# A hybrid recurrent decoder layer on one core: the first norm's squares on TensorE, the S5 tables in the opening, the S5 sums on all partitions

## The chip, the cores and the metric

One core of a Trainium2 chip runs the whole kernel. The metric is device microseconds of one execution, taken as the median of several runs. Shares and rows come from one profiled execution of the same program. Its engines are TensorE (PE, with its weight loads shown as PEld), VectorE (DVE), ScalarE (ACT), GpSimd (POOL) and SyncE (SP), which issues the DMAs.

## The reference

One decoder layer is computed for 1024 new positions of a prompt and for 8 single new tokens (1032 columns, features on the partitions). What matters here is the first half of the layer:

```
mod = silu(c) @ ada_w + ada_b                   # six parts of 1024: sh1, sc1, g1, sh2, sc2, g2
hn = x * rsqrt(mean(x*x) + eps) * norm1_g * (1 + sc1) + sh1
proj = hn @ w_in                                # 1024 x 1536: lru_x, lru_gate, s5_u
conv  = width-4 causal convolution of lru_x;  hs = gated real scan of conv (RG-LRU)
S5: 32 groups of 16 channels, each with one 64-dim complex diagonal state
  bu = Bbar u;  h[t] = abar * h[t-1] + bu[t]  (complex);  y = Re(C h) + d*u;  gelu, GLU
merged = [rmsnorm(hs * gelu(lru_gate)), rmsnorm(s5)];  x += g1 * (merged @ w_out)
```

Then follow a second modulated norm, a SwiGLU block of width 2816, and the final norm. States at the end of the sequence are outputs too.

## The kernel before, in words

Every fp32 product of the projections is made of three matmuls: a weight and an activation are each split into a high and a low part (`hnh`, `hnl`, `wh`, `wl`; lines 142 to 144), and the columns go in three pieces of 344. TensorE's instructions run in the order in which the code issues them, in the whole kernel.

**The opening** (lines 593 to 683) has its order written out by hand for every engine. It loads x in eight 128-row blocks and the scale part of `ada_w` in four quarters. For each pair of blocks (loop `i`, `d = 2 * i`), ACT and DVE split two columns of weights (`split_w01`) and form the modulated x (`stage`: ACT makes `hnh`, DVE makes `hnl`, POOL the eight token columns). ACT squares x (`square`, line 546). TensorE runs the products of these blocks with the first two column tiles of `w_in` (`first`) and the dot product that gives the next quarter of the scale (`ada_dot`, `ada_sum` in `scale_out`). The norm's factor is applied after the product, so the sum of squares is only needed near the end: POOL adds squares into `sqs[0]` in the loop (`add_square`), DVE does the last three adds, and `rstd_sums` sums over partitions with four TensorE matmuls against ones, one for each strip of 258 columns, into one of the two `small` PSUM banks. ACT takes the root and DVE the reciprocal. The steps of small S5 tables (`s5_powers`, some 80 tiny instructions) are pumped in between on DVE.

**The units** (from line 1089). Behind the opening come 30 units of 24 matmuls: one column tile of `w_in` times one third of the columns. `at(i, fn, ...)` hangs other work in front of unit `i`. DVE, ACT, POOL and SP are there ordered by a planner that works with estimated costs; TensorE keeps the order of the code. The S5 half goes in four tiles `f_`, with `STARTS = (4, 9, 14, 19)`: input tables, output tables (`s5_out_tables`) and the rotation `et` (`s5_rot`, on POOL) before the start; then `s5_turn`, `s5_drive` in two halves one and two units later, `s5_toeplitz` two units later, and `s5_out` five and seven units later. The second drive calls `s5_state`: rotate, scan, rotate back, all on DVE. Where an S5 result changes from channels on partitions (two groups of 64) to real and imaginary rows on partitions, the last subtraction or addition was made on 64 partitions at a time, two instructions for each (`ost` and `xt`), and one 4-element instruction more for the final state (`fin`, line 940).

The rotation tables `etb` and `eta` are made on POOL in front of unit 1, by 42 tensor_tensor instructions and four memsets; `lru_decay_scale` (32 dependent DVE instructions on 128x4) stands in front of unit 4. Its results `cl` and `ncl` are first read after the last unit, by `lru_exp`.

From the last unit on: gates, scans and GLU, then the output projection, and from about a third of the span on the SwiGLU block, whose products are made with fewer multiplications (bank names X, Y, Z).

Of the kernel before, what the change touches and what calls it, by code (L numbers as in the profile page):

```python
# [9 lines left out]
F32 = mybir.dt.float32  # L10
# [3 lines left out]
ALU = mybir.AluOpType  # L14
# [4 lines left out]
P = 128  # L19
# [35 lines left out]
def body(ctx, tc, a, o):  # L55
# [12 lines left out]
    def tt(out, x, y, op, e=None):  # L68
        (e or V).tensor_tensor(out=out, in0=x, in1=y, op=op)  # L69

    def mul(out, x, y, e=None):
        tt(out, x, y, ALU.mult, e)

    def add(out, x, y, e=None):
        tt(out, x, y, ALU.add, e)
# [468 lines left out]
    def square(d):  # L544
        sqs.append(f(f"sq1_{d}", TT))
        S.activation(sqs[d], xs[d][:, 0:TT], AF.Square)

    def add_square(d, e=None):
        add(sqs[0], sqs[0], sqs[d], e)

    def first(d, m, cs=range(NC)):
        for c in cs:
            mm3(banks[m, c], wcols(w01[m], d), cols(hn[d], c), d == 0, d == DK - 1)
# [35 lines left out]
    def split_w01(i, m):  # L589
        wh, wl = (t.rearrange("p (k n) -> p k n", k=DK)[:, 2 * i:2 * i + 2] for t in w01[m])  # L590
        split(wh, wl, w01_raw[:, 2 * i:2 * i + 2, m])

    small_a = [s5_angles()]
    small_b = [s5_powers()]

# [28 lines left out]
    first(1, 1)  # L624
    scr_ = cp.tile([P, 3], F32, name="scr")
    scr, scr2, scr3 = (scr_[:, i:i + 1] for i in range(3))
    for i in range(1, 4):
        d = 2 * i
        split_w01(i, 0)
        split_w01(i, 1)  # L630
        stage(d)
        stage(d + 1)
        if i == 1:
            pump(small_a, 99)
            pump(small_b, B1)
        elif i == 2:
            S.activation(scr, epst, AF.Sqrt)
        for j in ((1,), (2, 3), (4,))[i - 1]:
            add_square(j, G)
        if i < 3:  # L640
            sb = ada_dot(s_raw[i + 1], f"s{i + 1}")
        first(d, 0)
        square(d)
        if i < 3:
            scale_out(i + 1, *sb)
        square(d + 1)
        first(d, 1)
        first(d + 1, 0)
        if i < 3:
            first(d + 1, 1)  # L650
        if i < 3:
            pump(small_b, B0)
    add(sqs[6], sqs[6], sqs[5])
    add(sqs[6], sqs[6], sqs[7])
    add_square(6)
    split_in2 = split_w(w_in[2], "in2", pool=fp, tags=("F", "F"))
    for c in range(NC):
        evac(0, c, banks[0, c], True)
# [4 lines left out]
    rsb = dict(enumerate(sh_raw))  # L663
    rb1 = f("rb1", TT)
    bank20 = in_bank("in2_0", 0)
    r1 = rstd_sums((sqs[0],), D, "n1", TT, 4, f)
    for _ in steps(bank20, split_in2, [in_cols(hn[k], 0) for k in range(DK)]):
        pass
    pump(small_b, B2)
# [60 lines left out]
    def behind_states():  # L730
        return tc.issue_after(state_ends[-1]) if state_ends else nullcontext()

    etb = sp.tile([P, 2, 16, 16], F32, name="etb")
    eta = sp.tile([P, 2, 16, 8], F32, name="eta")

    def tpl(name):
        return sp.tile([P, 4, P], F32, tag="tpl", bufs=1, name=name)

    def s5_rot_tables(tab, k0, n):
        G.memset(tab[:, 0, :, 0:1], 1.0)  # L740
        G.memset(tab[:, 1, :, 0:1], 0.0)
        m = 1
        for k in range(n):
            er = rot[:, 0, k0 + k].unsqueeze(2).to_broadcast([P, 16, m])
            ei = rot[:, 1, k0 + k].unsqueeze(2).to_broadcast([P, 16, m])
            lo_, hi_ = tab[:, :, :, 0:m], tab[:, :, :, m:2 * m]
            for o_, x, y, op in ((0, er, ei, ALU.subtract), (1, ei, er, ALU.add)):
                w = tpl(f"te{k0}_{k}_{o_}").rearrange("p a b -> p (a b)")[:, 0:16 * m]
                w = w.rearrange("p (q m) -> p q m", q=16)
                mul(hi_[:, o_], lo_[:, 0], x, G)  # L750
                mul(w, lo_[:, 1], y, G)
                tt(hi_[:, o_], hi_[:, o_], w, op, G)
            m *= 2


    fin = sp.tile([P, 2, 16, 9], F32, name="fin")

    def s5_fin():
# [47 lines left out]
    def s5_out_tables(f_):  # L806

        q0 = 4 * f_
        cr, ci = sq[f_]["bc"][:, 1, 0], sq[f_]["bc"][:, 1, 1]
        awr = apw[:, 0, q0:q0 + 4].unsqueeze(3).to_broadcast([P, 4, 9, 16])  # L810
        awi = apw[:, 1, q0:q0 + 4].unsqueeze(3).to_broadcast([P, 4, 9, 16])
        crb = cr.unsqueeze(2).to_broadcast([P, 4, 9, 16])
        cib = ci.unsqueeze(2).to_broadcast([P, 4, 9, 16])
        ost = sp.tile([P, 8, 144], F32, tag="ost", bufs=2, name=f"ost{f_}")
        ov = ost.rearrange("p (q g) k -> p q g k", g=2)
        for ri, x, y in ((0, crb, cib), (1, cib, crb)):
            w = [t4(f"cw{ri}{i}_{f_}") for i in range(2)]
            wv = [t.rearrange("p q (j c) -> p q j c", j=9) for t in w]
            mul(wv[0], awr, x)
            mul(wv[1], awi, y)  # L820
            for g2 in range(2):
                h = slice(g2 * 64, g2 * 64 + 64)
                if ri == 0:
                    sub(ov[0:64, :, g2], w[0][h], w[1][h])
                else:
                    stt(ov[64:128, :, g2], w[0][h], -1.0, ALU.mult, w[1][h], ALU.subtract)
        sq[f_].update(ost=ost)

    def s5_rot(f_):
# [82 lines left out]
    def s5_state(f_):  # L912

        q0, pr = 4 * f_, sq[f_]
        vt, et = pr["vt"], pr["et"]
        add(fin[:, :, q0:q0 + 4, 1:9], fin[:, :, q0:q0 + 4, 1:9], vt[:, :, :, 0:8], G)
        w = [t4(f"rw{i}_{f_}")[:, :, 0:P] for i in range(3)]
        vr, vi = vt[:, 0, :, 8:136], vt[:, 1, :, 8:136]
        mul(w[0], et[:, 0], vr)
        mul(w[1], et[:, 1], vi)  # L920
        add(w[0], w[0], w[1])
        mul(w[1], et[:, 0], vi)
        mul(w[2], et[:, 1], vr)
        sub(w[1], w[1], w[2])
        for ri in range(2):
            for q in range(4):
                V.tensor_tensor_scan(out=vt[:, ri, q, 8:136], data0=mag8[:, q0 + q:q0 + q + 1].to_broadcast([P, P]),
                                     data1=w[ri][:, q], initial=0.0, op0=ALU.mult, op1=ALU.add)
        xt_ = sp2[0].tile([P, 8, 136], F32, tag="xt", bufs=1, name=f"xt{f_}")
        G.memset(xt_[:, :, 0:1], 0.0)  # L930
        nc.sync.dma_start(out=xt_[:, :, P:136], in_=a["h0s"][:, 8 * f_:8 * f_ + 8])
        xv = xt_.rearrange("p (q g) k -> p q g k", g=2)
        for ri, x, y, op in ((0, vr, vi, ALU.subtract), (1, vi, vr, ALU.add)):
            w = [t4(f"dw{ri}{i}_{f_}")[:, :, 0:P] for i in range(2)]
            mul(w[0], et[:, 0], x)
            mul(w[1], et[:, 1], y)
            for g2 in range(2):
                h = slice(g2 * 64, g2 * 64 + 64)
                tt(xv[64 * ri:64 * ri + 64, :, g2, 1:P], w[0][h, :, 0:P - 1], w[1][h, :, 0:P - 1], op)
            pr["last"] = V.tensor_tensor(out=fin[:, ri, q0:q0 + 4, 0:1], in0=w[0][:, :, P - 1:P],  # L940
                                         in1=w[1][:, :, P - 1:P], op=op)
            state_ends.append(pr["last"].ins)
        pr["xt"] = xt_

    def s5_out(f_, half):
# [97 lines left out]


    R0, R1 = 4, 1.12
    STARTS = (4, 9, 14, 19)
    IT, OT, RT, TZ, DA, DB, OA, TN, OB = 5, 0, 1, 2, 1, 2, 3, 1, 2
    CLOSE = 27
    before, mids = {}, {}
# [19 lines left out]
    at(2, bias_dot)  # L1069
    mids[1] = {1: [(rest_out, (3,))]}  # L1070
    mids[2] = {0: [(first_done, ())]}
    at(4, pump, [lru_decay_scale()], 99)
    for j in range(4, 20):
        i = int(R0 + R1 * (j - 4))
        at(i, rest_load, j)
        at(i + 2, rest_dot, j)
        at(i + 3, rest_out, j)
    at(1, s5_rot_tables, etb, 1, 4)
    at(1, s5_rot_tables, eta, 5, 3)
    at(3, s5_fin)  # L1080
    for f_ in range(4):
        i0 = STARTS[f_]
# [11 lines left out]
    for i, (m, c) in enumerate(SEQ):  # L1094
        for fn, args in before.get(i, []):
            fn(*args)
        if i == CLOSE:
            s5_end()
            s5ctx.close()
            hp = ctx.enter_context(tc.tile_pool(name="hp", bufs=15))  # L1100
            hpool.append(hp)
            gy_raw = [gy_load(f_) for f_ in range(4)]
        if (m, c) == (11, 2):
            wabf = wp.tile([P, 2, 4, P], F32, tag="wf", bufs=2, name="wabf")
            G.memset(wabf, 0.0)
            for j, nm in enumerate(("wa", "wx")):
                for e in range(2):
                    nc.sync.dma_start(out=wabf[e * 64:(e + 1) * 64, j, :, e * 64:(e + 1) * 64], in_=a[nm][e])
        if (m, c) == (11, 0):
            w_glu0 = load_w(a["w_glu"][0], "glu0")  # L1110
        if (m, c) == (2, 0):
            w_cur[3] = split_w(w_in[3], "in3")
        elif c == 2 and 3 <= m < 11:
            w_cur[m + 1] = load_w(a["w_in"][m + 1], f"in{m + 1}")
        b = in_proj(m, c, w_cur[m], mids.get(i, {})) if i else bank20
        if m < 4:
            u_out(m, c, b)
        elif m < 8:
            lx_out(m - 4, c, b)
        else:  # L1120
            gt_out(m - 8, c, b)
# [791 lines left out]
```

## Time and profile before

| | |
|---|---|
| median of 3 runs | 1166.81 us (1165.96 to 1168.72) |
| profiled execution: time, span | 1164.8 us, 1162.8 us |
| mean granted TensorE clock | 0.968 |
| PE, PEld busy | 94%, 90% |
| DVE, ACT, POOL busy | 73%, 43%, 39% |
| chain that ended last, shares | PE 70%, DVE 17%, ACT 5%, issue 4%, POOL 2%, DMA 1% |

A busy share is over the whole span; a busy matmul or DVE instruction may itself have been held up. The granted clock is in parts of the full one: 1.0 is 2.4 GHz, and a stretch whose mean lies between 0.5 and 1.0 was partly at 1.2 GHz. In rows of the timeline the first number is the start, the second the length, and the brackets hold the idle time of that engine before the row and what ended it.

### The profile page before, as it was taken

What the parts mean: (1) busy time and instruction counts of PE and PEld (TensorE: products, weight loads), DVE (VectorE), ACT (ScalarE), POOL (GpSimd) and SP (SyncE); (2) the same over time, 40 slices, a digit from 0 to 9 for tenths busy, and PEclk for the clock granted to TensorE, in tenths of its full rate; (3) what the DMA queues carried; (4) which work ended last, traced back from release to release, by engine and by line L of the source; (5) the groups of instructions that cost most, each with busy time, mean ns of one, the idle gap of its engine ahead of it and who ended that gap; (6) DMA issues with size and microseconds to landing.
All of it is one profiled execution on the core that took longest, in us unless ns stands there. A gap on an engine that the chain in (4) does not pass through costs nothing.

```text
span 1162.8 us, 21429 instructions
## 1 busy us (share of the span) xinstructions
PE 1088.8 (94%) x8480; PEld 1042.0 (90%) x8480; DVE 843.9 (73%) x1360; ACT 499.8 (43%) x948; POOL 456.3 (39%) x475
## 2 busy tenths in 40 slices
PE   7887889999987999899999999999999999999995
PEld 5776778896977998799999999999999999999995
DVE  6879799853978268986677687667645367778966
ACT  4433324327765145664445454445444521221253
POOL 3396645301020004574655575466432142233022
PEclk9898989899998999899999999999999999999998
DMA  9557455423042313052543344234313967459212
GB/s 344 183 155 206 156 171 146 154 77 107 19 130 89 130 56 110 19 193 90 192 182 129 109 182 155 101 146 182 128 56 102 350 259 303 171 202 294 89 54 93
DMA packets 90627, 174.92 MB, mean 150 GB/s; under 512 B 18720, under 2 KB 54304, under 8 KB 90528
## 3 DMA queue, kind: packets, MB, share of 16 engines
q1 hardware_dynamic: 90528, 173.57, 43.1%
q8 instruction: 66, 1.08, 0.4%
q14 instruction: 33, 0.27, 0.1%
HBM read 126.56 MB, written 46.98 MB: 149 GB/s over the span
## 4 chain that ended last, share of the span: by engine, by line
PE 70%; DVE 17%; ACT 5%; issue 4%; POOL 2%; DMA 1%; SPq 0%; DVEq 0%; ACTq 0%; POOLq 0%
PE X L1510 9%; PE X L1511 9%; PE X L1512 9%; PE Y L1510 5%; PE Y L1511 5%; PE Y L1512 5%; PE o L1308 2%; PE o L1309 2%; PE o L1310 2%; PE Z L1511 2%; PE Z L1512 2%; PE Z L1510 2%; DVE rw L69 1%; PE in L142 1%; PE in L143 1%
## 5 line engine op out<-in xcount | busy, mean ns | idle before, releaser
L69 POOL TENSOR_TENSOR u<-u,p 128x258 f32<-128x258 f32 x44 | 41.9, 953 | 125.2 <-ACT u L1562 115.8
L142 PE MATMUL in<-hnh,wh_in 128*128 128x344 f32 (+1 forms) x240 | 83.1, 346 | 0.0
L143 PE MATMUL in<-hnl,wh_in 128*128 128x344 f32 (+1 forms) x240 | 80.1, 334 | 0.0
L144 PE MATMUL in<-hnh,wl_in 128*128 128x344 f32 (+1 forms) x240 | 80.1, 334 | 0.0
L69 POOL TENSOR_TENSOR st_d<-wf_d 128x256 f32<-128x256 f32 x32 | 26.2, 838 | 111.6 <-PE X L1512 42.7
L69 POOL TENSOR_TENSOR sa_g<-wf_g 128x512 f32<-128x512 f32 x11 | 14.8, 1344 | 123.1 <-PE o L1310 91.4
L69 DVE TENSOR_TENSOR acc<-X,acc 128x258 f32<-128x258 f32 x128 | 49.9, 420 | 10.4 <-PE X L1512 10.2
L142 PEld LDWEIGHTS in<-hnh,wh_in 128*128 128x128 f32 x240 | 48.2, 201 | 2.9 <-issue 2.9
L143 PEld LDWEIGHTS in<-hnl,wh_in 128*128 128x128 f32 x240 | 48.1, 200 | 0.0
L144 PEld LDWEIGHTS in<-hnh,wl_in 128*128 128x128 f32 x240 | 47.7, 199 | 0.0
L1562 ACT ACTIVATE u<-X 128x258 f32<-128x258 f32 x88 | 33.1, 381 | 31.4 <-PE X L1512 31.4
L69 DVE TENSOR_TENSOR hs<-v,hs 128x516 fp32r<-128x516 f32 x32 | 46.1, 1458 | 0.6 <-ACT hs L1380 0.6
L1309 PE MATMUL o<-ls,wh_s 128*128 128x258 f32 x128 | 37.4, 292 | 5.6 <-DVE ls L69 5.6
L1308 PE MATMUL o<-hs,wh_s 128*128 128x258 f32 x128 | 37.3, 291 | 0.0
L1310 PE MATMUL o<-hs,wl_s 128*128 128x258 f32 x128 | 37.3, 291 | 0.0
L1308 PE MATMUL o<-hl,wh_l 128*128 128x258 f32 x128 | 36.6, 286 | 0.0
L69 POOL TENSOR_TENSOR acc<-acc,rbf 128x388 f32<-128x388 f32 x10 | 11.9, 1218 | 62.9 <-ACT rbf L201 51.1
L87 DVE SCALAR_TENSOR_TENSOR xz<-o,mod,xz 128x258 f32<-128x258 f32 (+1 forms) x32 | 15.2, 480 | 29.2 <-PE o L1310 25.6
L1310 PE MATMUL o<-hl,wl_l 128*128 128x258 f32 x128 | 36.1, 282 | 0.0
L1309 PE MATMUL o<-ll,wh_l 128*128 128x258 f32 x128 | 36.0, 282 | 0.0
L69 DVE TENSOR_TENSOR acc<-Y,acc 128x258 f32<-128x258 f32 x64 | 26.7, 424 | 10.4 <-PE Y L1512 9.5
L69 POOL TENSOR_TENSOR v<-u 128x516 f32<-128x516 f32 x16 | 21.3, 1332 | 32.5 <-DVE u L69 32.5
(1656 smaller groups left out, 4820.5 us busy)
## 6 DMA issues: line engine op xcount, KB each, us to landing
ht<-hs SPq DMA_DIRECT2D x48, 516.0 KB, 3.2
db<-ht SPq DMA_DIRECT2D x48, 516.0 KB, 8.9
ad<-ada SPq DMA_DIRECT2D x48, 512.0 KB, 6.2
wf_g<-w_gu SPq DMA_DIRECT2D x22, 512.0 KB, 3.9
wf_u<-w_gu SPq DMA_DIRECT2D x22, 512.0 KB, 3.4
wf_d<-w_dn SPq DMA_DIRECT2D x16, 512.0 KB, 4.2
wf_in<-w_in SPq DMA_DIRECT2D x10, 512.0 KB, 3.8
x<-xt SPq DMA_DIRECT2D x8, 516.0 KB, 7.8
```

Source lines behind the costliest of these rows:

```text
L69: (e or V).tensor_tensor(out=out, in0=x, in1=y, op=op)
L87: V.scalar_tensor_tensor(out=out, in0=x, scalar=s, in1=y, op0=op0, op1=op1)
L142: PE.matmul(ps, lhsT=wh, rhs=xh, start=first, stop=False)
L143: PE.matmul(ps, lhsT=wh, rhs=xl, start=False, stop=False)
L144: PE.matmul(ps, lhsT=wl, rhs=xh, start=False, stop=last)
L1308: PE.matmul(b, lhsT=wh, rhs=xh, start=half == 0 and k == 0, stop=False)
L1309: PE.matmul(b, lhsT=wh, rhs=xl, start=False, stop=False)
L1310: PE.matmul(b, lhsT=wl, rhs=xh, start=False, stop=half == 1 and k == 3)
L1510: PE.matmul(b, lhsT=wh, rhs=xh, start=first and k == 0, stop=False, skip_group_check=True)
L1511: PE.matmul(b, lhsT=wh, rhs=xl, start=False, stop=False, skip_group_check=True)
L1512: PE.matmul(b, lhsT=wl, rhs=xh, start=False, stop=k == nk - 1, skip_group_check=True)
L1562: S.activation(k[name], b[bank], AF.Copy)
```

## The change

Six edits. The squares are summed by TensorE: `square_sum(d)` issues the four strip matmuls for each of the eight blocks and accumulates them in one bank, `pc1`, taken at the head of the loop; POOL's five and DVE's three adds are gone. The 42 table instructions and their memsets go from unit 1 to the end of the opening's loop. `s5_out_tables` and `s5_state` add or subtract on all 128 partitions (in place, three scratch tiles in rotation) and ACT copies the two halves to where they belong; the final state is copied by POOL. The first S5 tile starts at unit 5. `lru_decay_scale` goes from unit 4 to unit 27. DMAs are neither added nor taken away; those of the first S5 tile (`kd`, `tm`, `h0s`, `yd`) go one unit later with it, all but its `u` and `bc` loads.

```diff
-    def add_square(d, e=None):
-        add(sqs[0], sqs[0], sqs[d], e)
+    def square_sum(d):
+        for j in range(4):
+            PE.matmul(pc1[32 * j:32 * j + 32, 0:CH], lhsT=ones[:, 0:1].to_broadcast([P, 32]),
+                      rhs=sqs[d][:, j * CH:j * CH + CH], start=d == 0, stop=d == DK - 1, tile_position=(0, 32 * j),
+                      skip_group_check=True)
...
+    pc1 = small("pc_n1")
     for i in range(1, 4):
...
-        for j in ((1,), (2, 3), (4,))[i - 1]:
-            add_square(j, G)
         if i < 3:
             sb = ada_dot(s_raw[i + 1], f"s{i + 1}")
         first(d, 0)
+        square_sum(d - 2)
+        square_sum(d - 1)
         square(d)
...
-    add(sqs[6], sqs[6], sqs[5])
-    add(sqs[6], sqs[6], sqs[7])
-    add_square(6)
+    s5_rot_tables(etb, 1, 4)
+    s5_rot_tables(eta, 5, 3)
...
-    r1 = rstd_sums((sqs[0],), D, "n1", TT, 4, f)
+    square_sum(6)
+    square_sum(7)
+    S.activation(pc1[:, 0:CH], pc1[:, 0:CH], AF.Sqrt, bias=epst, scale=1.0 / D)
+    r1 = f("rs_n1", CH), CH, 32
+    V.reciprocal(r1[0], pc1[:, 0:CH])
...
 (s5_out_tables)
+        w = [t4(f"cw{i}_{f_}") for i in range(3)]
         for ri, x, y in ((0, crb, cib), (1, cib, crb)):
-            w = [t4(f"cw{ri}{i}_{f_}") for i in range(2)]
+            w = w if ri == 0 else [w[2], w[1]]
...
+            tt(w[0], w[0], w[1], (ALU.subtract, ALU.add)[ri])
             for g2 in range(2):
                 h = slice(g2 * 64, g2 * 64 + 64)
-                if ri == 0:
-                    sub(ov[0:64, :, g2], w[0][h], w[1][h])
-                else:
-                    stt(ov[64:128, :, g2], w[0][h], -1.0, ALU.mult, w[1][h], ALU.subtract)
+                S.activation(ov[64 * ri:64 * ri + 64, :, g2], w[0][h], AF.Copy, scale=(1.0, -1.0)[ri])
 (s5_state)
+        w = [t4(f"dw{i}_{f_}")[:, :, 0:P] for i in range(3)]
...
-            w = [t4(f"dw{ri}{i}_{f_}")[:, :, 0:P] for i in range(2)]
+            w = w if ri == 0 else [w[2], w[1]]
             mul(w[0], et[:, 0], x)
             mul(w[1], et[:, 1], y)
+            end = V.tensor_tensor(out=w[0], in0=w[0], in1=w[1], op=op)
+            state_ends.append(end.ins)
             for g2 in range(2):
                 h = slice(g2 * 64, g2 * 64 + 64)
-                tt(xv[64 * ri:64 * ri + 64, :, g2, 1:P], w[0][h, :, 0:P - 1], w[1][h, :, 0:P - 1], op)
-            pr["last"] = V.tensor_tensor(out=fin[:, ri, q0:q0 + 4, 0:1], in0=w[0][:, :, P - 1:P],
-                                         in1=w[1][:, :, P - 1:P], op=op)
-            state_ends.append(pr["last"].ins)
+                S.activation(xv[64 * ri:64 * ri + 64, :, g2, 1:P], w[0][h, :, 0:P - 1], AF.Copy)
+            G.tensor_copy(fin[:, ri, q0:q0 + 4, 0:1], w[0][:, :, P - 1:P])
...
-    STARTS = (4, 9, 14, 19)
+    STARTS = (5, 9, 14, 19)
...
-    at(4, pump, [lru_decay_scale()], 99)
...
-    at(1, s5_rot_tables, etb, 1, 4)
-    at(1, s5_rot_tables, eta, 5, 3)
...
         if i == CLOSE:
+            pump([lru_decay_scale()], 99)
             s5_end()
```

## Rows read from the trace of the kernel before

**Rows 1.** Busy time by stretch: start:end, length, engines' busy time, granted clock, DMA.
```profile
12.00:62.00 50.00, 44.07 (x284) 37.17 (x288) 37.15 (x84) 26.31 (x43) 20.68 (x52) 0.86 0.67 250
62.00:110.00 48.00, 38.80 (x284) 34.55 (x277) 43.26 (x97) 17.13 (x47) 42.31 (x75) 0.89 0.68 198
110.00:250.00 140.00, 123.45 (x926) 109.01 (x926) 121.67 (x208) 42.84 (x105) 58.02 (x60) 0.93 0.45 142
250.00:270.00 20.00, 20.00 (x127) 19.57 (x126) 7.51 (x10) 5.29 (x7) 0.20 (x1) 1.00 0.59 159
350.00:1162.80 812.80, 784.99 (x6436) 776.76 (x6428) 570.57 (x869) 343.69 (x658) 319.98 (x266) 0.99 0.42 149
```

**Rows 2.** Timeline of PE in the opening: start, length, instruction, idle before it.
```profile
25.96 0.61 PE L238 MATMUL pa_s<-ct,adas_s 128*128 128x9 f32 x4 [1.54 <-ACT adas_s L230]
28.08 0.49 PE L142 MATMUL u<-hnh,wh_in 128*128 128x344 f32 x1
28.37 0.49 PE L143 MATMUL u<-hnl,wh_in 128*128 128x344 f32 x1
...
37.38 0.66 PE L143 MATMUL u<-hnl,wh_in 128*128 128x344 f32 x1 [3.56 <-DVE hnl L87]
...
48.02 0.32 PE L143 MATMUL u<-hnl,wh_in 128*128 128x344 f32 x1
48.17 0.32 PE L144 MATMUL u<-hnh,wl_in 128*128 128x344 f32 x1
...
53.88 0.64 PE L181 MATMUL pc_n<-sq,ones 128*32 128x258 f32 x8
```

**Rows 3.** Timeline of DVE in the opening.
```profile
22.26 2.42 DVE L84 TENSOR_SCALAR tmp<-tmp 128x128 f32<-128x128 f32 x1
...
33.20 2.93 DVE L69 TENSOR_TENSOR wl_in<-w_raw,wh_in 128x256 fp32r<-128x256 f32 x2
...
44.96 0.75 DVE L69 TENSOR_TENSOR wl_in<-w_raw,wh_in 128x256 fp32r<-128x256 f32 x2
...
48.02 3.90 DVE L69 TENSOR_TENSOR sq<-sq,sq 128x1032 f32<-128x1032 f32 x3
```

**Rows 4.** Timeline of POOL in the opening.
```profile
22.04 2.45 POOL L69 TENSOR_TENSOR sq<-sq,sq 128x1032 f32<-128x1032 f32 x1
...
30.86 4.99 POOL L69 TENSOR_TENSOR sq<-sq,sq 128x1032 f32<-128x1032 f32 x2
```

**Rows 5.** Groups of POOL by shape, 58 to 92 us: count, busy us, mean ns.
```profile
L69 POOL TENSOR_TENSOR sst<-apw,pk 128x128 f32<-128x128 f32 x4 | 1.7, 430 | 0.0
...
L69 POOL TENSOR_TENSOR te<-etb,rot 128x16 f32<-128x16 f32 x2 | 0.4, 224 | 0.1
```

**Rows 6.** Waits, 60 to 250 us: waiter, releaser, us in total, times, longest.
```profile
PE pv L903 <- ACT kt L867: 4.9, 1, 4.9
...
PE py L955 <- DVE mod L69: 4.3, 2, 4.1
...
PE pv L903 <- POOL te L69: 3.6, 1, 3.6
```

**Rows 7.** Groups of DVE by shape, 62 to 250 us.
```profile
L69 DVE TENSOR_TENSOR xt<-dw,dw 64x508 f32<-64x508 f32 x16 | 15.4, 960 | 0.3
...
L69 DVE TENSOR_TENSOR dw<-et,vt 128x512 f32<-128x512 f32 x16 | 10.7, 687 | 0.2
L87 DVE SCALAR_TENSOR_TENSOR ost<-cw,cw 64x576 f32<-64x576 f32 x8 | 7.4, 930 | 0.2
L69 DVE TENSOR_TENSOR ost<-cw,cw 64x576 f32<-64x576 f32 x8 | 7.2, 897 | 0.1
...
L87 DVE SCALAR_TENSOR_TENSOR tmp<-tmp,tmp 128x4 f32<-128x4 f32 x18 | 6.2, 347 | 0.3
...
L940 DVE TENSOR_TENSOR fin<-dw,dw 128x4 f32<-128x4 f32 x8 | 4.2, 528 | 0.2
```

**Rows 8.** Timeline of ACT, one copy out of PSUM.
```profile
143.23 0.51 ACT L959 ACTIVATE yg<-py 128x408 f32<-128x408 f32 x1 [1.11 <-PE py L957]
```

More of the change, by code (lines that the diff above doesn't have):

```diff
@@ L591, in split_w01, with tpl, s5_rot_tables @@
         split(wh, wl, w01_raw[:, 2 * i:2 * i + 2, m])
+    etb = sp.tile([P, 2, 16, 16], F32, name="etb")
+    eta = sp.tile([P, 2, 16, 8], F32, name="eta")
+    def tpl(name):
+        return sp.tile([P, 4, P], F32, tag="tpl", bufs=1, name=name)
+    def s5_rot_tables(tab, k0, n):
+        G.memset(tab[:, 0, :, 0:1], 1.0)
+        G.memset(tab[:, 1, :, 0:1], 0.0)
+        m = 1
+        for k in range(n):
+            er = rot[:, 0, k0 + k].unsqueeze(2).to_broadcast([P, 16, m])
+            ei = rot[:, 1, k0 + k].unsqueeze(2).to_broadcast([P, 16, m])
+            lo_, hi_ = tab[:, :, :, 0:m], tab[:, :, :, m:2 * m]
+            for o_, x, y, op in ((0, er, ei, ALU.subtract), (1, ei, er, ALU.add)):
+                w = tpl(f"te{k0}_{k}_{o_}").rearrange("p a b -> p (a b)")[:, 0:16 * m]
+                w = w.rearrange("p (q m) -> p q m", q=16)
+                mul(hi_[:, o_], lo_[:, 0], x, G)
+                mul(w, lo_[:, 1], y, G)
+                tt(hi_[:, o_], hi_[:, o_], w, op, G)
+            m *= 2
     small_a = [s5_angles()]
@@ L731, in behind_states @@
         return tc.issue_after(state_ends[-1]) if state_ends else nullcontext()
[L733 to L753, printed above, removed]
     fin = sp.tile([P, 2, 16, 9], F32, name="fin")
```

## The prediction

> **What bounds the kernel now.** I read the busy time by stretch first [rows 1]. From 350 us on PE is busy 785.0 of 812.8 us at a clock of 0.99, and nothing of the change lies there; the last units (250 to 270) are all PE as well. The three stretches that the change touches are looser. In the opening, 12 to 62 us, PE stands idle 50.0 - 44.1 = 5.9 us and its clock is 0.86. From 62 to 110, where the first S5 tile is made, it is idle 9.2 us at 0.89 with DVE busy 43.3 of 48 and POOL 42.3. From 110 to 250, with the other three tiles, it is idle 16.6 us at 0.93 with DVE busy 121.7 of 140. So PE waits for DVE and POOL in all three, and what those gain can come back to PE; after 250 us a microsecond won earlier is kept, since the last units and all behind them only shift.
>
> Then the timelines, to see what the waits are. In the opening two stand out: 1.54 us before 25.96 and 3.56 us before 37.38 [rows 2]. Behind each the clock is at its lower level: one projection matmul then follows the last after 0.29 us (28.08 to 28.37), and after 0.15 to 0.16 us at the higher (48.02 to 48.17). I counted steps between such matmuls of 0.26 to 0.31 us: 33 from 12 to 62, 26 from 62 to 110, 30 from 110 to 250, each 0.13 us too long: 4.3, 3.4 and 3.9 us. The cause of both waits shows on DVE and POOL. The 128x128 DVE instruction at 22.26 takes 2.42 us, just while POOL adds squares (22.04, 2.45 us), and the two weight splits at 33.20 take 2.93 us inside POOL's two adds (30.86, 4.99 us), where the same pair takes 0.75 us at 44.96 with POOL quiet [rows 3, 4].
>
> The Trainium skill has a rule for this (SBUF — State Buffer, "Who interferes with whom"): a DVE instruction with two SBUF inputs and a GpSimd instruction that reads SBUF share a port pair, which is held for a whole instruction while the other blocks. The two pairs of rows agree (2.42 beside 2.45 us). The rule also speaks against this change: it carries 42 POOL instructions into the opening. What it would make of the time is the first rival.
>
> **The parts.**
>
> *Squares on TensorE.* Five POOL adds go, and with them the two blocks on DVE: 2.42 us becomes at most the 0.75 of a quiet pair, so the angles, the sines behind them and `adas_s` come about 2 us earlier, and the 1.54 us wait is gone; the splits win 2.93 - 0.75 = 2.2 us, and with the 2 us from before that covers the 3.56 us. What goes with the waits is the lower clock behind them. Gross 1.54 + 3.56 + 4.3 = 9.4 us. Against it stand eight sums for one: a row of four strip matmuls takes 0.64 us (53.88) [rows 2], so 7 x 0.64 = 4.5 us more on PE, all on its one queue. Two of the sums fall where PE would wait for `adas_s` in any case, but I leave the full price. DVE's last three adds (3.90 us) end before PE wants them, as PE is busy without a break from 47 us, so they bring nothing. `pc1` holds one `small` bank through the loop; the other is held by a product bank, and no one else asks for one there. Net -4.9 us.
>
> *Tables in the opening.* 42 POOL instructions on 16 to 128 elements. One takes 224 ns at 16 elements and 430 ns at 128 [rows 5]: together between 42 x 0.224 = 9.4 and 42 x 0.430 = 18.1 us; by size (12 at 16, 12 at 32, 12 at 64, 6 at 128, between the two) I take 12. They start behind POOL's part of the last `stage` and lie beside DVE's twelve pumped steps, two splits and `hnl` of block 6, about 16 DVE instructions that PE's next product waits for. Bounds: nothing, or all 12 us on that path. Each DVE instruction may wait for the rest of one table instruction, half of 0.2 us, so 16 x 0.1 = 1.6 us; I take +1.5. The rest runs while PE has its queue full. The `apr` copies on POOL now wait behind the tables; they are read only by the units' input tables. Opening: -4.9 + 1.5 = -3.4 us.
>
> *62 to 110 us.* The tables leave this stretch: POOL's 42.3 us lose about 12 and more, since many of them were held up there. The decay scale leaves it too: 18 of its 32 instructions alone are 6.2 us, mean 347 ns [rows 7], so 32 x 0.347 = 11 us at most and, at the 0.17 us of the shortest, 5 at least; I take 10. It goes to unit 27, where DVE is busy 7.5 of 20 us [rows 1], and its result is wanted only after the last unit: no cost, and if that cover were gone, up to 11 us in the gates. The two waits here are 3.6 us for the first drive (the row names a POOL table, but `u` came with a DMA behind POOL's queue) and 4.9 us for a bank that ACT emptied late, as ACT stood behind a DVE result [rows 6]. The first tile one unit later gives both some 4 us more (24 matmuls at 0.16). Idle and clock together are 9.2 + 3.4 = 12.6 us. What is late next is the first state, whose tables now are closer to the second tile's (4 units, not 5). I take -9; bounds 0 and -12.6.
>
> *S5 sums on all partitions.* `xt` and `fin` are 15.4 + 4.2 = 19.6 us of DVE in 24 instructions; 8 full-width ones take their place, at the 687 ns of a `dw` product 5.5 us: -14.1. `ost` is 7.4 + 7.2 = 14.6 us in 16; 8 at the same length are 7.3: -7.3 [rows 7]. That is 21.4 us, 5.4 for each tile, for 32 ACT copies on 64 partitions. ACT takes 0.51 us for 408 columns [rows 8], so at most 0.72 for 576 and 0.64 for 508: 22 us on an engine that is busy 43 of 140 us. As a chain, a sum and two copies (0.7 + 1.4) are as long as two sums and the `fin` (2 x 0.96 + 0.53): nothing there. Added waits: the next user of a scratch tile waits for the copies, but with three in rotation that is a tile used two steps before; and behind ACT's copies stand its PSUM evacuations, for which PE waits (the last rival). `fin` on POOL is two small copies a tile, read by the last DMA alone.
>
> What it gives from 110 to 250 us: PE's idle time and lower clock are 16.6 + 3.9 = 20.5 us. DVE loses three quarters of 21.4 = 16 us of its 121.7. If DVE alone set the pace, the stretch would shrink by 16 / 0.87 = 18 us at its share of 87%; if the waits come from the order (DVE does a state or a convolution before the small read that frees PE's bank, as in the 4.3 us of `py` for `mod` [rows 6]) or from POOL's rotations, which stay, by nothing. I take a third of 20.5: -6.5, nearer the lower end, because a faster PE gives DVE less time for each unit.
>
> **Sum:** -3.4 - 9 - 6.5 = -18.9 us on the profiled execution's 1164.8 us: 1145.9. The median of the runs is 2.0 us above it, so 1147.9.
>
> **Rivals.**
>
> 1. *The tables hold the opening.* By the rule above, each of the 12 us may stand in front of the DVE chain to block 6 and 7. For it: 2.42 us at 22.26 behind one POOL add. Against: the table instructions are short, and PE has 27 matmuls queued there. Opening -4.9 + 12 = +7.1; in all -8.4: 1158.4.
>
> 2. *DVE and POOL stay the pace.* The waits come back a unit later, since tile 0 now lies closer to tile 1 and `et` has one buffer. For it: DVE is at 87 to 90% and PE's clock falls after each wait. Opening -3.4, units -3: 1160.4.
>
> 3. *The waits were all DVE's load.* -4.9 in the opening, -12.6, -18: -35.5, 1131.3. Against: it needs every wait to go at once.
>
> 4. *Slower: ACT's queue.* 16 pairs of copies wait on ACT for a DVE sum, and banks that PE needs are emptied behind them. The 4.9 us wait for `kt` [rows 6] is just that: ACT stood behind a DVE result. At that price four such waits (19.6 us) eat the gain, and from the fifth on it is slower: six give 29.4 - 18.9 = +10.5, 1177.3. With four the change does nothing, 1167. Against: ACT copies are issued by the planner in the order in which it expects inputs, and ACT has room.
>
> **How the numbers follow.** The forecast 0.50 (its own range 1140 to 1156), rival 1 0.14, rival 2 0.13, rival 3 0.09, rival 4 0.08, and 0.06 for its middle, no change. A measurement of this kernel can tell about 0.2% (2.3 us) from no change. Faster: 0.50 + 0.14 + 0.13 + 0.09 = 0.86; same 0.06; slower 0.08. The range reaches from just above rival 3 to just above rival 2, 1132 to 1163, and leaves out rival 4, the middle and half of rival 3.
>
> **What would show it.** No DVE instruction of some 2 us beside a POOL add before 36 us, and PE without the waits at 26 and 37; eight rows of 0.64 us of `pc_n`; POOL's tables before the first unit, and no second wait of PE before block 6. In the first tile, no 3.6 and 4.9 us. On DVE `xt` and `ost` gone and 21 us less, on ACT 32 copies of 0.6 to 0.7 us. The gates begin about 19 us earlier, and from there to the end both traces have the same length. I am wrong if the opening ends no earlier than 62 us, if PE's idle time from 110 to 250 stays near 16, or if PE waits for evacuations that stand behind the new copies.

## The result, and the profile after

The changed kernel takes 1149.64 us (median of 4 runs, 1147.02 to 1154.45) against 1167.07 us of the kernel before beside it: a ratio of 0.9867, interval 0.9847 to 0.9887, or 15.5 us less by the ratio (the two medians lie 17.4 us apart). Its profiled execution took 1147.02 us with a span of 1145.2 us at a mean clock of 0.980 (before 1162.8 us, 0.968).

Busy time by stretch of the changed kernel, columns as in [rows 1]:

```profile
12.00:62.00 50.00, 49.99 (x388) 39.38 (x389) 30.74 (x90) 29.87 (x50) 29.74 (x89) 1.00 0.70 261
62.00:110.00 48.00, 40.29 (x288) 35.66 (x287) 35.44 (x99) 18.87 (x48) 21.81 (x39) 0.92 0.67 200
110.00:250.00 140.00, 128.44 (x968) 115.83 (x967) 111.57 (x184) 62.36 (x133) 61.88 (x67) 0.95 0.49 152
350.00:1145.20 795.20, 774.57 (x6351) 768.39 (x6351) 556.94 (x851) 332.87 (x639) 320.76 (x266) 0.99 0.42 151
```

PE has no gap left in the opening (44.07 busy of 50 became 49.99). Its granted clock became 1.00 from 0.86, but the first part of this is not a gain: up to about 20 us the matmuls of the changed kernel still follow each other after 0.28 to 0.29 us, the step of the lower level, though the clock reads 1.00 there; before, the same stretch read 0.50 (14 to 16 us). From 62 to 110 us POOL's busy time has halved and DVE's fell by 7.8 us, yet PE is busy only 1.5 us more; from 110 to 250 it is busy 5 us more, with DVE down 10.1 and ACT up 19.5 us. The stretches are the same in time and not in work: they hold 4 and 42 matmuls more than before.

Timeline of PE in the opening, answering to [rows 2]; two rows of sums are one line here:

```profile
16.07 0.49 PE L142 MATMUL u<-hnh,wh_in 128*128 128x344 f32 x1
16.36 0.49 PE L143 MATMUL u<-hnl,wh_in 128*128 128x344 f32 x1
...
27.08 1.08 PE L551 MATMUL pc_n<-sq,ones 128*32 128x258 f32 x16
28.08 0.61 PE L238 MATMUL pa_s<-ct,adas_s 128*128 128x9 f32 x4
...
35.60 1.08 PE L551 MATMUL pc_n<-sq,ones 128*32 128x258 f32 x16
```

No bracket stands behind them: both waits are gone. Two rows of sums hold PE's queue for 1.00 us (27.08 to 28.08), 0.50 us a row.

Timelines of DVE and then of POOL in the opening, answering to [rows 3, 4]; the last three lines of each are work behind the opening:

```profile
24.99 0.23 DVE L84 TENSOR_SCALAR tmp<-tmp 128x128 f32<-128x128 f32 x1
...
31.51 0.76 DVE L69 TENSOR_TENSOR wl_in<-w_raw,wh_in 128x256 fp32r<-128x256 f32 x2
...
39.25 0.83 DVE L69 TENSOR_TENSOR wl_in<-w_raw,wh_in 128x256 fp32r<-128x256 f32 x2
40.00 2.47 DVE L87 SCALAR_TENSOR_TENSOR hnl<-x,g,hnh 128x1024 fp32r<-128x1024 f32 x2
...
60.12 3.26 DVE L69 TENSOR_TENSOR up<-up,rb 128x1024 f32<-128x1024 f32 x2
...
63.93 1.24 DVE L69 TENSOR_TENSOR bb<-fr,bc 128x64 f32<-128x64 f32 x1
...
65.23 1.28 DVE L69 TENSOR_TENSOR bb<-fr,bc 128x64 f32<-128x64 f32 x1
```

```profile
40.12 1.25 POOL L69 TENSOR_TENSOR etb<-etb,rot 128x16 f32<-128x16 f32 x1
41.32 1.24 POOL L69 TENSOR_TENSOR te<-etb,rot 128x16 f32<-128x16 f32 x1
...
62.06 1.29 POOL L69 TENSOR_TENSOR et<-et,ew 128x512 f32<-128x512 f32 x1
...
64.04 1.05 POOL L69 TENSOR_TENSOR ew<-eta,etb 128x512 f32<-128x512 f32 x1
65.17 1.26 POOL L69 TENSOR_TENSOR et<-et,ew 128x512 f32<-128x512 f32 x1
```

The 128x128 instruction takes 0.23 us instead of 2.42, the pairs of splits 0.76 and 0.83 us instead of 2.93.

Waits of PE from 62 to 270 us, columns as in [rows 6]:

```profile
PE py L963 <- DVE mod L69: 6.4, 3, 3.2
PE pmod L238 <- ACT pst L861: 3.9, 2, 2.7
PE ppt L858 <- DVE mod L69: 3.7, 1, 3.7
PE pa_b L225 <- DVE shf L69: 3.6, 1, 3.6
```

(`pv`, `kp` and `py` are banks of an S5 tile: its drive, its Toeplitz table and its output; `mod` and `shf` are parts of the modulation that DVE reads out of PSUM.) The first tile's two waits of [rows 6], 3.6 and 4.9 us for `pv`, are not there. A wait of 3.6 us for `shf` is new: it was 0.66 us before. The largest part of what is left, 10.1 us, is PE waiting for DVE to read a bank (`mod`).

Groups of DVE and then of ACT by shape from 62 to 250 us, answering to [rows 7]:

```profile
L945 DVE TENSOR_TENSOR dw<-dw,dw 128x512 f32<-128x512 f32 x8 | 7.0, 876 | 0.1
L69 DVE TENSOR_TENSOR cw<-cw,cw 128x576 f32<-128x576 f32 x8 | 6.7, 842 | 0.0
...
L87 DVE SCALAR_TENSOR_TENSOR tmp<-tmp,tmp 128x4 f32<-128x4 f32 x18 | 3.1, 172 | 0.3
```

```profile
L833 ACT ACTIVATE ost<-cw 64x576 f32<-64x576 f32 x16 | 10.9, 684 | 24.0 <-DVE cw L69 23.8
L949 ACT ACTIVATE xt<-dw 64x508 f32<-64x508 f32 x16 | 10.0, 626 | 17.4 <-DVE dw L945 17.2
```

DVE's 34.2 us of `xt`, `fin` and `ost` became 13.7, and 32 copies cost ACT 20.9 us. The third line of DVE is the decay scale, still here: its rows run from 69.5 to 90.7 us, as they ran from 69.2 to 97.9 before.

Three marks cut each trace into pieces that hold the same work: the first scale dot on PE, the broadcast sums `pb_n` that end the opening, and the first gate matmul (`r`), then the first `o` of the output projection.

| us | first dot | `pb_n` | first gate | first `o` | span |
|---|---|---|---|---|---|
| before | 6.5 | 59.5 | 268.6 | 346.6 | 1162.8 |
| after | 8.5 | 55.5 | 254.6 | 329.5 | 1145.2 |

From dot to `pb_n` that is 53.0 and 47.0 us (-6.0), from `pb_n` to the gates 209.1 and 199.1 (-10.0), from there to `o` 78.0 and 74.9 (-3.1), and behind it 0.5 us less. The first dot itself came 2.0 us later; over the traces of this study it lies between 6.3 and 8.5 us.

How far one trace can be trusted shows where kernels have the same code. The opening, from dot to `pb_n`, takes 53.0 to 53.6 us in the five kernels that have neither squares nor tables changed, 46.5 to 47.8 in the four that have both, 46.2 to 47.6 in the three that have the squares alone. Behind the first `o`, where no edit lies, all fourteen traces take 815.7 to 819.8 us. So a difference of 1.4 us between two openings, or of 4 us behind the first `o`, is no price of an edit.

### The profile page after: what moved, and what is told of

Its sections match the earlier page's. It is cut to its first block, busy times and chain, and to the rows that moved or that the text cites. A ratio compares the mean times of both kernels' runs of the same rounds, so it can differ in the third digit from the quotient of the medians.

```text
span 1145.2 us, 21550 instructions
## 1 busy us (share of the span) xinstructions
PE 1086.1 (95%) x8536; PEld 1036.7 (91%) x8536; DVE 813.3 (71%) x1333; ACT 518.7 (45%) x980; POOL 449.6 (39%) x479
## 4 chain that ended last, share of the span: by engine, by line
PE 77%; DVE 12%; ACT 4%; issue 3%; DMA 2%; SPq 1%; POOL 1%; DVEq 0%; ACTq 0%; POOLq 0%
PE X L1516 10%; PE X L1517 9%; PE X L1518 9%; PE Y L1516 5%; PE Y L1517 5%; PE Y L1518 5%; PE o L1315 2%; PE o L1314 2%; PE o L1316 2%; PE Z L1518 2%; PE Z L1517 2%; PE Z L1516 2%; PE in L142 2%; PE in L143 2%; PE in L144 2%
## 5 line engine op out<-in xcount | busy, mean ns | idle before, releaser
L1568 ACT ACTIVATE u<-X 128x258 f32<-128x258 f32 x88 | 33.1, 381 | 31.1 <-PE X L1518 31.1
```

Of the source, the lines that this page charges most:

```text
L1568: S.activation(k[name], b[bank], AF.Copy)
```

## The experiments

Each kernel was timed in five rounds beside the kernel before (1164.85 to 1165.40 us); ratios are to it, with their 95% intervals.

**One part alone, on the kernel before.** The edits are those parts of the diff in "The change", each by itself.

Squares on TensorE:

```diff
-        add(sqs[0], sqs[0], sqs[d], e)
+            PE.matmul(pc1[32 * j:32 * j + 32, 0:CH], lhsT=ones[:, 0:1].to_broadcast([P, 32]), ...
```

> The kernel before with the squares summed by TensorE and nothing else. My theory: the opening is held by POOL's adds, so without them PE's waits of 1.54 and 3.56 us go, the clock stays at the higher level, the first spread of the norm's factor starts 3 to 6 us earlier, and 4 to 6 us are left at the end: about 1162 us. Rival: what the opening gains is waited away in the S5 stretch, where DVE is the pace: 1165 to 1167 us with a longer stretch from the spread to the gates.

Measured 1158.79 us, 0.9947 (0.9934 to 0.9959): -6.1 us. The opening took 47.6 us from dot to `pb_n`, -5.4.

Tables in the opening:

```diff
+    s5_rot_tables(etb, 1, 4)
+    s5_rot_tables(eta, 5, 3)
     split_in2 = split_w(w_in[2], "in2", pool=fp, tags=("F", "F"))
...
-    at(1, s5_rot_tables, etb, 1, 4)
-    at(1, s5_rot_tables, eta, 5, 3)
```

> The kernel before with the 42 table instructions in the opening and nothing else. My theory: behind POOL's adds the tables cost the opening 1 to 2 us and free POOL and DVE at 62 to 90 us of some 12 us, which shortens the wait of the first drive (3.6 us): 1163 to 1165 us. Rival (the shared access of DVE and POOL): the tables hold the DVE chain to blocks 6 and 7, the opening ends 3 to 7 us later and the kernel is slower than before, 1168 to 1172 us.

Measured 1172.37 us, 1.0065 (1.0053 to 1.0077): +7.5 us, slower. The opening was only 1.2 us longer (54.2), within the spread above; from `pb_n` to the gates it took 213.6, 4.5 us more. POOL's timeline of this kernel:

```profile
64.53 0.32 POOL L69 TENSOR_TENSOR eta<-eta,te 128x64 f32<-128x64 f32 x1
64.79 3.22 POOL L453 COPY apr<-apw 128x32 f32<-128x32 f32 x8
```

Behind POOL's adds the tables end at 64.8 us, and the `apr` copies, which began at 58.20 before, end at 68. The first tile's tables wait for them. The waits of PE, 60 to 270 us, of the same kernel:

```profile
PE pv L905 <- ACT kt L869: 6.2, 1, 6.2
PE pv L905 <- DMA u<-ud: 5.3, 1, 5.3
...
PE pa_b L225 <- DVE shf L69: 2.0, 1, 2.0
```

These three were 4.9, 3.6 and 0.7 us: 4.3 us more. Other waits shrank, so PE's idle time in the whole stretch grew only from 25.8 to 27.2 us; the other 3.1 of the 4.5 us are the same matmuls taking longer (186.4 us for 183.4, clock 0.91 for 0.93):

```profile
61.00:274.60 213.60, 186.44 (x1345) 165.75 (x1342) 171.33 (x313) 66.84 (x164) 93.83 (x129) 0.91 0.50 152
```

S5 sums on all partitions:

```diff
-                tt(xv[64 * ri:64 * ri + 64, :, g2, 1:P], w[0][h, :, 0:P - 1], w[1][h, :, 0:P - 1], op)
+            end = V.tensor_tensor(out=w[0], in0=w[0], in1=w[1], op=op)
...
+                S.activation(xv[64 * ri:64 * ri + 64, :, g2, 1:P], w[0][h, :, 0:P - 1], AF.Copy)
```

> The kernel before with the S5 sums on all partitions (ACT copies the halves) and nothing else. My theory: DVE has some 20 us less from 100 to 245 us, of which PE gets a third: 4 to 8 us, 1159 to 1163 us. Rival 1: PE's waits come from the order in which DVE does its work, not from its load: within 1 us of before. Rival 2: the new copies stand in front of evacuations on ACT, and PE waits for ACT more than before: 1168 us or more.

Measured 1160.92 us, 0.9965 (0.9951 to 0.9979): -3.9 us, with the first tile's waits (4.2 and 3.6 us) still there.

First tile one unit later:

```diff
-    STARTS = (4, 9, 14, 19)
+    STARTS = (5, 9, 14, 19)
```

> The kernel before with the first S5 tile one unit later and nothing else. My theory: the waits of 3.6 and 4.9 us in the first tile go with their stretch at the lower clock, and some of it is given back at the second tile: 4 to 7 us less, 1160 to 1163 us. Rival: the waits only come one unit later: 1165 to 1168 us.

Measured 1166.73 us, 1.0011 (1.0000 to 1.0021): +1.9, nothing won. Both waits are gone, but another came at the first tile's `kp`, in the waits of PE from 62 to 270 us of this kernel:

```profile
PE py L955 <- DVE mod L69: 7.9, 3, 4.6
PE py L957 <- DVE xt L69: 6.2, 5, 3.2
PE kp L864 <- ACT vt L907: 6.1, 1, 6.1
```

And the units behind run at a low clock, with DVE nearly full (busy time by stretch of the same kernel; before, with five units between the first two tiles, DVE was busy 33.1 and 39.6 us here, the clock 0.91 and 0.87):

```profile
140.00:180.00 40.00, 33.51 (x227) 30.76 (x228) 35.96 (x57) 12.60 (x33) 21.00 (x21) 0.84 0.46 134
180.00:220.00 40.00, 33.12 (x247) 28.49 (x249) 39.13 (x55) 9.88 (x25) 21.84 (x22) 0.87 0.54 167
```

The decay scale at unit 27:

```diff
-    at(4, pump, [lru_decay_scale()], 99)
...
         if i == CLOSE:
+            pump([lru_decay_scale()], 99)
```

> The kernel before with only lru_decay_scale moved from unit 4 to unit 27 in the code. Theory 1 (only a rank in the plan): DVE does it later by some us among the first units, 0 to 3 us less, 1162 to 1165 us. Theory 2 (the place of the decay scale is the rest of the sum): 5 us less or more, 1160 us or below.

Measured 1166.36 us, 1.0008 (0.9999 to 1.0016): nothing.

The parts add up to about nothing, +0.4 us, and together they give -15.5: they depend on one another.

**One part undone, on the changed kernel.** Each edit is the reverse of one above.

```diff
+        for j in ((1,), (2, 3), (4,))[i - 1]:
+            add_square(j, G)
...
-        square_sum(d - 2)
-        square_sum(d - 1)
```

> The changed kernel with the adds of squares back on POOL and DVE. The parts so far, one at a time against before: squares -6.1, tables +7.5, sums -3.9, start +1.9 us, which add to -0.6 where the whole change gave about -15.5. Theory of an interaction: POOL's adds and the tables stand in one queue and in front of DVE's chain, so the tables cost only while the adds are there; without the squares edit the kernel is then as bad as tables alone plus the rest, 1164 to 1170 us, some 15 us over the changed kernel. Rival (the parts just add, and something else made the difference): 6 us over the changed kernel, 1155 to 1157 us.

Measured 1164.33 us, 0.9992 (0.9981 to 1.0004): all of the gain is gone. The opening took 53.5 us, and the stretch behind 206.9. As in the tables alone, POOL comes to the tables late, behind its adds: they end at 64.1 us. The tables alone (1.0065) and the pair below (0.9917) multiply to 0.9981, close to this kernel.

```diff
-    s5_rot_tables(etb, 1, 4)
...
+    at(1, s5_rot_tables, etb, 1, 4)
```

> The changed kernel with the table instructions back in front of unit 1. Theory: the tables in the opening are worth something only now that POOL is empty there; POOL's 42 instructions and their hold on DVE return to 60 to 85 us and PE waits there again: 4 to 9 us over the changed kernel, 1153 to 1159 us. Rival (tables in the opening cost as they did alone): faster than the changed kernel, 1142 to 1146 us.

Measured 1147.28 us, 0.9848 (0.9832 to 0.9865): 2 us better than the changed kernel by the medians, with intervals that meet. The opening took 46.2 us, 0.8 less than the changed kernel's, and the wait for `shf` is 0.6 us instead of 3.6. The opening's difference is within the spread of equal openings.

```diff
-            tt(w[0], w[0], w[1], (ALU.subtract, ALU.add)[ri])
...
-                S.activation(ov[64 * ri:64 * ri + 64, :, g2], w[0][h], AF.Copy, scale=(1.0, -1.0)[ri])
+                if ri == 0:
+                    sub(ov[0:64, :, g2], w[0][h], w[1][h])
...
```

> The changed kernel with the S5 sums back on 64 partitions at a time. Theory: they are worth 4 us alone and the same here, 1153 to 1155 us. Rival (with the opening clean, PE presses on DVE sooner and DVE's load counts more): 6 to 10 us, 1156 to 1160 us.

Measured 1162.96 us, 0.9985 (0.9971 to 0.9999): nearly all of the gain gone, though the sums alone brought a quarter of it.

```diff
-    STARTS = (5, 9, 14, 19)
+    STARTS = (4, 9, 14, 19)
```

> The changed kernel with the first S5 tile back at unit 4. Theory (as it was alone, the later start brings nothing): 1147 to 1150 us, no slower than the changed kernel. Rival (with POOL empty the first tile is ready a unit later, and starting at unit 4 makes PE wait for it): 1153 to 1158 us.

Measured 1152.09 us, 0.9896 (0.9882 to 0.9909): +2.7 us. The two waits of the first tile are not back: nothing of the 3.6 us, and of the 4.9 us only this (waits of PE, 60 to 110 us):

```profile
PE pv L910 <- ACT kt L874: 0.4, 1, 0.4
```

So in the changed kernel it is not the later start alone that removes them. The squares alone (3.6 and 4.0 us), the sums alone (3.6 and 4.2) and the decay scale alone (4.7 and 3.0) keep both; that leaves the tables made early by a POOL without the adds, which no run shows by itself.

```diff
+    at(4, pump, [lru_decay_scale()], 99)
...
-            pump([lru_decay_scale()], 99)
```

> The changed kernel with lru_decay_scale back in front of unit 4. In the changed kernel the planner still puts the decay scale at 69.5 to 90.7 us, where it was before (69.2 to 97.9), so theory 1: only its rank in the plan changed, and the time is within 2 us of the changed kernel, 1148 to 1152 us. Theory 2 (rest of the sum): the four other edits, undone or done one at a time, leave 5 to 15 us unexplained, and the place of the decay scale is what is left: 1155 to 1163 us.

Measured 1150.21 us, 0.9870 (0.9855 to 0.9885): no difference (+0.3 us by the ratios).

**A wait taken away.** With the tables back at unit 1, `py` still waits for DVE to read the bank of `mod` (waits of PE in that kernel, 60 to 270 us):

```profile
PE py L961 <- DVE mod L69: 7.5, 2, 3.9
```

ACT copies that product out of PSUM, so that the bank is free at once:

```diff
+        if part or h:
+            pe_ = pt
+            pt = cp.tile([P, 64], F32, tag="pmc", bufs=2, name=f"pmc{part}_{h}")
+            S.activation(pt, pe_[:, 0:64], AF.Copy)
```

> The changed kernel with the tables back in front of unit 1, and with ACT copying the small product of ada_out out of its PSUM bank, so that DVE's addition (the tile mod) reads the copy. In the profile without the copy PE waits 7.5 us in two waits of py for mod, behind a DVE that does the state or the convolution first. Theory (the waits left are the order on DVE, not its load): these go, 3 to 8 us below 1147.3, so 1139 to 1144 us. Rival (ACT's queue or DVE's load hold the same banks anyway): PE waits elsewhere, 1145 to 1149 us.

Measured 1147.63 us, 0.9851 (0.9833 to 0.9868): nothing. Waits of PE, 60 to 270 us:

```profile
PE pmod L238 <- ACT pst L863: 5.2, 2, 3.2
PE kp L873 <- ACT vt L916: 4.2, 2, 3.6
PE kp L873 <- issue: 3.8, 1, 3.8
```

The wait for `mod` is gone and others took its place: PE's idle time from `pb_n` to the gates went from 18.7 to 19.4 us. My reading, not shown by a run, is that the bank was only where a lag of the S5 chain showed.

**Two parts together, on the kernel before:** the sums and the later start, the two edits as above.

> The kernel before with two parts of the change together: the S5 sums on all partitions and the later start of the first S5 tile. Alone they gave -3.9 and +1.9 us. Theory (they need each other: the later start clears the first tile's waits for u and kt, about 8 us, but leaves the first two tiles four units apart, which fits only a lighter VectorE): about -9 to -12 us, 1153 to 1157 us, with about 198 to 201 us from the last broadcast sum of the opening to the gates (209.1 before). Rival (the parts just add): -2 us, 1162 to 1164 us, with 205 to 207 us in that stretch.

Measured 1155.98 us, 0.9917 (0.9898 to 0.9935): -9.2 us, where the sum of the two is -2.0. From `pb_n` to the gates it took 199.7 us. This stretch holds the same 1344 or 1345 matmuls in every kernel, so one row of each tells where its length lies (columns as in [rows 1]). Before:

```profile
59.50:268.60 209.10, 183.35 (x1344) 164.31 (x1341) 171.73 (x313) 66.91 (x164) 102.95 (x154) 0.93 0.51 155
```

The sums alone, and the later start alone:

```profile
60.40:265.50 205.10, 183.27 (x1344) 163.72 (x1341) 157.60 (x289) 86.46 (x196) 104.71 (x162) 0.93 0.53 158
```

```profile
61.50:271.50 210.00, 182.75 (x1345) 163.47 (x1342) 169.80 (x313) 66.70 (x164) 100.12 (x154) 0.92 0.52 154
```

The two together, the changed kernel, and the changed kernel without the sums:

```profile
60.40:260.10 199.70, 177.16 (x1344) 159.62 (x1341) 155.91 (x289) 86.27 (x196) 105.01 (x162) 0.96 0.53 162
```

```profile
55.50:254.60 199.10, 179.82 (x1345) 161.33 (x1342) 153.53 (x289) 86.97 (x196) 90.19 (x120) 0.95 0.54 164
```

```profile
54.20:267.40 213.20, 185.66 (x1345) 166.75 (x1342) 171.34 (x313) 66.99 (x164) 85.51 (x111) 0.90 0.51 153
```

Length less PE's busy time is PE's idle time: 25.8 us before, 21.8 with the sums, 27.3 with the later start, 22.5 with both, 19.3 after, 27.5 without the sums. Two thirds of what the pair wins here is matmuls that got shorter (183.35 to 177.16, clock 0.93 to 0.96), one third is idle time. In the changed kernel it is the other way about: of its 10.0 us, 3.5 are shorter matmuls (179.82) and 6.5 idle time. The sums take 14.1 us off DVE. With the first two tiles four units apart and the old sums DVE is busy 36.0 and 39.1 of 40 us from 140 to 220 (above). With the new ones, in the kernel with both parts, DVE has room in the second half, the clock is higher throughout, and the 80 us hold 552 matmuls and not 474:

```profile
140.00:180.00 40.00, 32.84 (x258) 29.11 (x257) 37.87 (x54) 15.81 (x32) 27.91 (x27) 0.91 0.52 158
180.00:220.00 40.00, 36.84 (x294) 32.16 (x293) 33.05 (x53) 19.49 (x47) 17.15 (x22) 0.96 0.54 171
```

By the ratios the squares and the pair make up the whole change: 0.9947 x 0.9917 = 0.9864, against 0.9867. The changed kernel without its tables, which is these parts and the decay scale, gives 0.9848 (0.9832 to 0.9865). Tables and decay scale are left with nothing that these runs can tell from zero.

## Why the prediction was right, and where it was not

The time is near the forecast (1149.6 for 1147.9), and the forecast's case is what happened: the waits named went, and no new one ate the gain. But the terms inside it moved against each other, so that the sum comes this near is in part luck.

- **The opening** was right in kind, and better than forecast: -6.0 us for -3.4. Squares: both waits and the lower clock behind them are gone, -5.4 alone (forecast -4.9). Counted by one rule, the steps between projection matmuls of 0.26 to 0.31 us fell from 36 to 11 here (from 27 to 15 and from 33 to 14 in the next two stretches). Part of the rest is the price of the sums: 0.50 us a row and not 0.64, so 7 rows cost 3.5 and not 4.5. Two readings were off: the kernel before has four POOL adds, not five, and the two of 30.86 us hold a third DVE instruction as well, the 128x16 `fr` at 30.87, which takes 2.42 us and 0.18 in the changed kernel. Tables: +0.8 (changed kernel against itself without them) and +1.2 (tables alone) for the +1.5; equal openings differ as much, so the runs show only that they cost little.
- **Rival 1** did not come. Of POOL and DVE it was POOL that paid: its 16-element instructions at 40.12 and 41.32 took 1.25 and 1.24 us beside DVE's two `hnl` (2.47 us), where the same shape takes 0.23 to 0.24 alone, while DVE's splits beside the tables took 0.83 us for 0.76. The Trainium skill (SBUF — State Buffer, "Who interferes with whom") calls the port pair that the two engines share an exclusive lock. These rows agree: the price of a block is about the length of the holder's instruction, so short ones cost their neighbour little. Of the prediction's two pairs of rows only the splits read two SBUF inputs; the instruction of 22.26 reads one and was held all the same, 2.42 us for 0.23.
- **62 to 110 us, the decay scale: the step that failed.** "It goes to unit 27" was read off the code. DVE's order is the planner's, and it still ran from 69.5 to 90.7 us. The 10 us that I took off DVE did not go that way; its instructions did get cheaper, 172 ns for 347, beside a POOL half as busy. Alone (+1.0) and undone (+0.3) it is nothing.
- **62 to 110 us, the tables.** That POOL loses 12 us and more was right (42.3 to 21.8); that this is worth time was not: undone, the change is 2 us faster by the medians. A POOL that is early starts the first rotation early. Its 512-wide products then lie beside DVE's `up` pair (60.12), which takes 3.26 us where it took 2.06 in the kernel before, and beside the two `bb` behind it, 1.24 and 1.28 us for 0.23 and 0.34. That is 3.2 us in front of `shf`, and PE waits 3.6 us for 0.66. With the tables back at unit 1 the three take 2.04, 0.23 and 0.33 us and the wait is 0.6.
- **62 to 110 us, the later start.** Both first-tile waits went, as forecast, and the later start alone does remove them; but they are gone without it too once the other edits are in, where it is worth 2.7 us. That the second tile is then closer was named in the prediction and given no price; alone it costs all that the start wins. With the lighter DVE the pair wins 9.2 us for the 2.0 of its parts, and that the two need each other was not seen.
- **110 to 250 us.** DVE's share was nearly right: 20.5 us less in these groups for the 21.4, as the new sums take 0.84 and 0.88 us and not 0.69; but DVE as a whole lost 18.2 from `pb_n` to the gates (171.7 to 153.5), and 14.1 with the sums alone, since other instructions on it got longer (in the changed kernel the four 128x1032 `xc` take 1.36 us for 0.81). ACT's copies were priced right (0.68 and 0.63 us for 0.72 and 0.64). For the units as a whole I had -15.5, and it is -10.0.
- **Behind the gates** I had no change, and it is -3.1 us up to the first `o`; this made good part of the miss, and nothing in the prediction stands for it. Half, 1.6 us, is in the clock (below). The other half is a wait of PE behind the gates, before and after; why it is shorter was not tried:

```profile
PE pb_l L199 <- DVE s5o L69: 1.7, 1, 1.7
PE pb_l L199 <- DVE s5o L69: 0.2, 1, 0.2
```

- **Rivals 2 to 4.** Waits did not come back (idle 25.8 to 19.3 us), nor did they all go at once. Of ACT's queue there is 0.9 us for `xt`, 0.4 for `vt` and 3.9 for `pst`, 5.2 us in all up to the gates, against 9.3 of waits for ACT before. What was slower was none of the rivals: the tables alone, by a cause that I had only as "the `apr` copies wait behind the tables" and priced at nothing.

Together: -18.9, 5.5 back in the units, 2.6 more in the opening, 3.1 and 0.5 more behind, and 2.0 for the later first dot: -17.6 us, by which the spans differ.

The best version run is the changed kernel with its tables at unit 1 (1147.28 us), though it and the changed kernel are not clearly apart. Why the tables alone cost 7.5 us is shown in part: 4.5 us lie between `pb_n` and the gates, with the first tile's longer waits. Of the rest of its trace, 1.2 us more in the opening, 1.5 less from the gates to `o` and 3.5 more behind it, the first and the last are within the spread of equal code, and all three are left open.

## What to carry to other kernels

Where several edits relieve the same chain, price them together: moving a stage later can be worth nothing until the engine that then bounds it is lighter, and the lighter engine little until the stage moves. Before a step is priced by where the code puts it, ask whether its engine follows the code's order at all, and what the engine that it leaves will start sooner. Where a clock falls behind waits, look at the length of the busy matmuls as well as at the idle time: here that was two thirds of the pair's gain and a third of the whole change's.

## What the runs showed of the hardware that was not expected

Behind the same wait the clock can fall or not. PE's wait in the gates ("PE i <- ACT r") is 2.90 us in the kernel before and 2.91 after. Before, the six microseconds behind it:

```profile
275.00:278.00 3.00, 3.00 (x8) 1.89 (x7) 1.25 (x2) 3.00 (x7) 0.00 (x0) 0.64 0.00 0
278.00:281.00 3.00, 3.00 (x10) 1.83 (x9) 1.12 (x1) 2.45 (x6) 0.00 (x0) 0.79 0.29 91
```

And after:

```profile
261.00:264.00 3.00, 3.00 (x12) 1.89 (x10) 1.27 (x2) 3.00 (x7) 0.00 (x0) 1.00 0.00 0
264.00:267.00 3.00, 3.00 (x12) 1.98 (x11) 1.09 (x1) 3.00 (x9) 0.66 (x1) 1.00 0.29 82
```

PE is busy throughout in all four, at a mean clock of 0.72 in one kernel and of 1.00 in the other: 6 x 0.28 = 1.7 us. The first six matmuls of `r` behind the wait take 3.05 us before and 1.90 after. From the first gate to the first `zb` all fourteen traces have one of two lengths: 18.4 to 18.5 us in eight, 16.9 to 17.0 in six. With the start alone it is the short one, with the start undone too, and with the decay scale undone the long one: no one part of the change sets it, and why it falls one way was not tried.
